# A hybrid trunk in fp32 on one core: five instead of four groups of a feed-forward by seven products, and loads, norms and low parts placed anew

## The chip, the core and the metric

One core of a Trainium2 chip. The time is the device time of one execution in microseconds (us), the median of several. TensorE (PE) multiplies, VectorE (DVE) adds and subtracts, ScalarE (ACT) copies and applies functions, GpSimd (POOL) does powers and some subtractions and issues DMAs, SyncE (SP) issues the loads.

## The reference

Sequence 512, width 1024, two layers. Layer 0 mixes with an mLSTM, layer 1 with a gMLP. Each layer is feed-forward, mixer, feed-forward, embedding; every step is a residual with a layer norm.

```python
D_MODEL = 1024; SEQ = 512; DEPTH = 2; FFN_HIDDEN = 2816; DN_ALPHA = (2.0 * DEPTH) ** 0.25
def swiglu_ffn(x, w_gu, w_d):
    g, u = jnp.split(x @ w_gu, 2, axis=-1)
    return (jax.nn.silu(g) * u) @ w_d
def gmlp_mixer(x, w_in, b_in, vn_g, vn_b, ws, bs, w_out):
    u, v = jnp.split(jax.nn.gelu(x @ w_in + b_in, approximate=False), 2, axis=-1)
    v = layer_norm(v, vn_g, vn_b).reshape(B, NB, GM_BLOCK, GM_GROUPS, GM_GDIM)
    ...
    s = jnp.einsum('gts,bnsgc->bntgc', ws_m, v) + bs.T[:, :, None]
    return (u * s.reshape(B, S, GM_WIDTH)) @ w_out
...
    for i in range(DEPTH):
        x = layer_norm(DN_ALPHA * x + 0.5 * swiglu_ffn(x, ffn1_wgu[i], ffn1_wd[i]), ln_g[i, 0], ln_b[i, 0])
        j = i // N_MIXERS
        if i % N_MIXERS == 0:
            mix = mlstm_mixer(x, ml_w_in[j], ml_b_in[j], ml_conv[j], ml_norm_g[j], ml_w_out[j])
        else:
            mix = gmlp_mixer(x, gm_w_in[j], gm_b_in[j], gm_vn_g[j], gm_vn_b[j], gm_ws[j], gm_bs[j], gm_w_out[j])
        x = layer_norm(DN_ALPHA * x + mix, ln_g[i, 1], ln_b[i, 1])
        x = layer_norm(DN_ALPHA * x + 0.5 * swiglu_ffn(x, ffn2_wgu[i], ffn2_wd[i]), ln_g[i, 2], ln_b[i, 2])
        ple = jax.nn.sigmoid(x @ ple_wg[i] + ple_bg[i]) * (p[i] @ ple_wp[i])
        x = layer_norm(DN_ALPHA * x + ple, ln_g[i, 3], ln_b[i, 3])
```

## The kernel before, in words

The activation x stays on the chip as `xt` (four token blocks of 128 tokens, t = 0 to 3, by 1024). For a matrix product over its columns a block is turned on PE (`turn_x`, four 128x128 transposes for each half into `xps`) and split into a high and a low part, `xh` and `xl`, in the type fp32r. Every product in fp32 is three products of such parts (`mm3`, lines 258 to 260): high by high, high by low, low by high. The norm behind the first feed-forward of a layer and behind a mixer is "deferred": only mean and scale are applied to `xt` (L535), gain and bias when a block is turned (`xf` on ACT). The others multiply with `g_bc` and add `b_bc` in two operations for each half (L538, L539).

The program is scheduled by hand: each engine runs its instructions in the order in which the code issues them.

`Weights` (`W`) holds one list of all weight tiles in the order of their use. `fill` takes them strictly in that order: it splits a loaded tile (`wraw`, or `wquarter` for the quarters of a group) into `whi` on ACT (L183) and `wlo` on DVE (L189), and stops at the first tile whose kind has no free buffer. The kinds are "main" (4 buffers), "extra" (2) and, in a feed-forward, "rows" (3). With `low="dma"` the low part is made by an ACT copy and an accumulating DMA of POOL (L186, L187), with `low=pool` by a subtraction on POOL. `release` frees a buffer and fills again; `release(later=True)` keeps it for a `refill`.

A feed-forward has 22 hidden blocks of 128 columns. Each takes two projections (`fps`, 24 matmuls of 512 columns), then silu, the product `hf` and its split. They go down to `xt` in chunks of 2, 4, 4, 4, 4, 4 blocks. The first 2 and the last 4 go plainly (`down`: for each token block two banks `dps`, 24 matmuls for each hidden block). Each chunk of four in the middle is a `Group`: its 2 by 2 product is made by seven products of quarters instead of eight (`product(r)`, 12 matmuls into two banks `gps`; even r uses one pair of banks, odd r the other), with `form()` making the sums of h on DVE and their split (`fhi`, `flo`), and `add()` adding a product's two banks to `xt`. The products of a group stand between the projections of the next chunk: each follows one projection. The weights of the products come as "rows" tiles, one behind each of the next chunk's projection tiles in `W`'s list.

Behind the last chunk `down` runs token block by token block: `residual` and `norm.stats` for both halves, then `norm.prepare` (aggregate, `rs`, a power on POOL) and `norm.scale`, and the turns of the block two places before. Turns of the last blocks are `hooks` that the next stage runs inside its first projections (`up_staged`).

At the start x's blocks and the first weights are loaded in turn. In the gMLP the v half is projected first (`gvps`, `up_tokens`), normed and split (`gvh`, `gvl`), then u (`gups`) and the mixing over tokens (`sps`). In the embedding a block is worked in `(t, e)` steps: `rest()` of one step runs behind the sigmoid of the next.

Of the kernel before, what the change touches and what calls it, by code (L numbers as in the profile page):

```python
# [16 lines left out]
P = 128  # L17
D = 1024
# [28 lines left out]
class Weights:  # L47
# [68 lines left out]
    def reserve(self, kind, n):  # L116

        js = [self.add_load(None, 1, kind) for _ in range(n)]
        self.held_raws[kind].extend(js)
        return js, [self.spare(kind) for _ in js]  # L120

    def spare(self, kind):
        return self.raw_pools[kind].tile([P, 1024], F32R, name="wquarter", tag="wquarter")

    def drop(self, js):
        for j in js:
            self.left[j] = 0
# [9 lines left out]
    def load(self, only=None):  # L137

        for kind, queue in self.queues.items():
# [3 lines left out]
            if queue and len(held) < self.raw_bufs.get(kind, 0) and only in (None, kind):  # L143
# [9 lines left out]
                for i in range(parts):  # L153
                    s = slice(i * a // parts, (i + 1) * a // parts)
                    self.nc.sync.dma_start(raw[:, s], ap[:, s])
# [72 lines left out]
def hybrid_trunk(ctx: ExitStack, tc, x, p, ln_g, ln_b, ffn1_wgu, ffn1_wd, ffn2_wgu, ffn2_wd,  # L228
# [80 lines left out]
    FFN_CHUNKS = [2, 4, 4, 4, 4, 4]  # L309
    LAST = len(FFN_CHUNKS) - 1  # L310
    turn_p = []

    def ffn_weights(wgu, wd, name, ple=False):
# [16 lines left out]
        for c, n in enumerate(FFN_CHUNKS):  # L330
            down_w = deque(forms(starts[c - 1]) if c > 1 else ())
            for i in range(2 * n):
                W.order.append(tiles[2 * starts[c] + i])
                if down_w:
                    W.order.append(down_w.popleft())
                if c == 1 and i == 1:
                    add_rows(wd, 0, n // 2, "rows")
# [166 lines left out]
    class Norm:  # L504
# [12 lines left out]
        def stats(self, t, i, n):  # L517

            if i == 0:
# [11 lines left out]
        def scale(self, t):  # L531
# [5 lines left out]
            for c in (slice(0, 512), slice(512, D)):  # L537
                vec.scalar_tensor_tensor(y[:, c], y[:, c], mean, self.g_bc[:, c], op0=OP.subtract, op1=OP.mult)  # L538
                vec.scalar_tensor_tensor(y[:, c], y[:, c], rstd, self.b_bc[:, c], op0=OP.mult, op1=OP.add)  # L539
# [42 lines left out]
    def down(hs, first, norm=None, low=(None,) * 4, between=None, lazy=False, defer=False):  # L582


        n = len(hs)
        ws, kinds = [], []

        def release(k):
            kind = "rows" if kinds[k] == "rows" else None
            if norm is None:  # L590
                W.release(kind=kind, low=low[k])
            elif kind == "rows":
                W.free[kind] += 1
            elif defer:
                W.release()
            else:
                W.release(later=lazy or bool(W.held))
# [3 lines left out]
        for t in range(TB):  # L601
            banks = [dn_bank("dps"), dn_bank("dps")]
            for k in range(n):
                if k == len(ws):
                    ws.append(W.take())
                    kinds.append(W.kind)
                if norm is not None and k == 1 and t:
                    norm.prepare(t - 1)
                    if t >= 2:
                        turn_x(t - 2, up_bank, (0,), norm)  # L610
                        if not norm.deferred:
                            turn_x(t - 2, up_bank, (1,), norm)
                    norm.scale(t - 1)
                if norm is not None and k == 2 and t >= 2 and norm.deferred:
# [12 lines left out]

            def finish(t=t, banks=banks):
                for half, ps in enumerate(banks):
                    residual(t, half, ps, first)  # L630
                    if norm is not None:
                        norm.stats(t, half, 2)
                if between is not None:
                    between(t)
                if norm is not None and t == TB - 1:
                    norm.apply(t)
                    set_hooks(norm)

            if defer and t == TB - 1:
                return finish  # L640
            finish()
            if first:
                run_affine()
# [8 lines left out]
    def up_staged(first=False):  # L652
# [37 lines left out]
    class Group:  # L690
# [5 lines left out]
        def __init__(self, h, pool):  # L696
            self.h, self.pool = h, pool
# [3 lines left out]
        def form(self):  # L701
# [4 lines left out]
            r = self.next_form  # L706
            if r == 7:
                return
            self.next_form += 1
# [22 lines left out]
        def add(self):  # L732
# [3 lines left out]
            for e, ps in enumerate(self.banks[r % 2]):  # L736
                residual(2 * i + e, j, ps, False)


    def ffn(layer, k, rows, prepare=None):  # L740
        with stage_pool("forms", 2) as fpool, stage_pool("quarters", Q_BUFS) as qpool, stage_pool("hpool", 2) as hpool:
            name = (layer, k)
            W.open_raw(name, qpool, Q_BUFS)
            reserved, hs = W.reserve(name, FFN_CHUNKS[0])
# [12 lines left out]
            pending = group = None  # L757
            for c, n in enumerate(FFN_CHUNKS):
                plain = c in (0, LAST)
                if c == 0:  # L760
                    hs = [halves(a) for a in hs]
                elif c == LAST:
                    assert not W.queues[name]
                    hs = []
                    if prepare is not None:
                        prepare()
                else:
                    h = hpool.tile([P, 4, SEQ], F32, name="h", tag="h")
                for i in range(2 * n):
# [8 lines left out]
                    else:  # L778
                        hf = tmp_tile("hf") if plain else h[:, b]
                        if c == LAST:  # L780
                            hs.append(halves(W.spare(name)))
                        vec.scalar_tensor_tensor(hf, sg, 0.5, ps, op0=OP.mult, op1=OP.mult)
                        if plain:
# [6 lines left out]
                    if (c, i) in ((0, 3), (1, 0)):  # L790
                        run_affine()
                    if i == 1 and pending is not None:
# [563 lines left out]
```

## Time and profile before

| | |
|---|---|
| median of 3 runs | 2259.32 us (2258.81 to 2259.34) |
| profiled execution | 2260.95 us, span 2259.1 us, mean granted clock 0.998 |
| PE busy | 2233.4 us, 99% of the span |
| DVE, ACT, POOL busy | 1448.7, 872.3, 121.2 us |
| DMA | 246.19 MB, mean 109 GB/s |

Rows of the time line read: start in us, duration, engine and line, operation, out<-in, sizes, how many like it in a row, and in brackets the idle time ahead with what ended it. Rows of waits read: who waits for what, then us in total, times, the longest. A row of windows has the stretch, its length, and the busy time and number of instructions of PE, PEld (weight loads), DVE, ACT and POOL, then the granted clock of PE, the DMA share and GB/s.

### The profile page before, as it was taken

The numbers are of one execution on the slowest core, as the hardware profiler recorded it, in microseconds if no ns is written. First come the engines' busy times: TensorE is split into PE (matmuls) and PEld (weight loads), VectorE is DVE, ScalarE is ACT, GpSimd is POOL, SyncE is SP. The second block draws the span as 40 slices with busy tenths as digits, with TensorE's granted clock in tenths as the row PEclk, the third lists the DMA queues.
The fourth block names the chain that finished last, engine by engine and source line by source line (L and its number), as shares of the span: only waits on it lengthen the run. The fifth ranks groups of instructions, "written<-read, shape, count | busy, mean of one in ns | idle before, by whom it ended". The sixth has DMA issues, their size and how long they took to land.

```text
span 2259.1 us, 26267 instructions
## 1 busy us (share of the span) xinstructions
PE 2233.4 (99%) x10623; PEld 1873.0 (83%) x10623; DVE 1448.7 (64%) x2083; ACT 872.3 (39%) x1226; POOL 121.2 (5%) x136
## 2 busy tenths in 40 slices
PE   8999999999999999999999999999999999999997
PEld 7888888888888888888888888888888888888886
DVE  4566667755555666666677566666666566666677
ACT  3333336454545433333254333335233352333332
POOL 1000000111111000000000000000021200000000
PEclk9999999999999999999999999999999999999999
DMA  7333223376684434331233322223223243332221
GB/s 236 104 96 100 94 84 103 78 175 126 145 163 102 147 112 142 101 103 66 94 122 125 121 91 87 91 94 117 89 94 103 75 137 98 129 112 85 84 84 56
DMA packets 192176, 246.19 MB, mean 109 GB/s; under 512 B 5380, under 2 KB 147844, under 8 KB 192056
## 3 DMA queue, kind: packets, MB, share of 16 engines
q1 hardware_dynamic: 165824, 211.83, 28.7%
q0 software_dynamic: 19616, 18.01, 5.6%
q10 hardware_dynamic: 6616, 14.69, 1.9%
q8 instruction: 83, 1.36, 0.2%
q14 instruction: 37, 0.30, 0.0%
HBM read 224.58 MB, written 2.11 MB: 100 GB/s over the span
## 4 chain that ended last, share of the span: by engine, by line
PE 89%; DVE 6%; ACT 2%; DMA 1%; issue 1%; POOL 0%; SPq 0%; POOLq 0%; ACTq 0%; DVEq 0%
PE fps L258 13%; PE fps L260 13%; PE fps L259 13%; PE gps L260 5%; PE gps L259 5%; PE gps L258 5%; PE dps L258 4%; PE dps L260 4%; PE dps L259 4%; DVE wlo L189 2%; PE vps L258 1%; PE zps L258 1%; PE zps L260 1%; PE vps L259 1%; PE vps L260 1%; PE zps L259 1%
## 5 line engine op out<-in xcount | busy, mean ns | idle before, releaser
L258 PE MATMUL fps<-xh,whi 128*128 128x512 f32 x1312 | 510.6, 389 | 0.0
L259 PE MATMUL fps<-xl,whi 128*128 128x512 f32 x1312 | 510.5, 389 | 0.0
L260 PE MATMUL fps<-xh,wlo 128*128 128x512 f32 x1312 | 510.4, 389 | 0.0
L189 DVE TENSOR_TENSOR wlo<-wraw,whi 128x1024 fp32r<-128x1024 f32 (+1 forms) x284 | 341.2, 1218 | 185.0 <-ACT whi L183 184.1
L183 ACT ACTIVATE whi<-wraw 128x1024 fp32r<-128x1024 f32 (+1 forms) x333 | 343.5, 1048 | 217.5 <-PE fps L259 103.1
L260 PEld LDWEIGHTS fps<-xh,wlo 128*128 128x128 f32 x1312 | 246.3, 188 | 51.1
L259 PEld LDWEIGHTS fps<-xl,whi 128*128 128x128 f32 x1312 | 246.3, 188 | 51.0
L258 PEld LDWEIGHTS fps<-xh,whi 128*128 128x128 f32 x1312 | 246.3, 188 | 50.9
L189 DVE TENSOR_TENSOR wlo<-wquarter,whi 128x1024 fp32r<-128x1024 f32 x112 | 137.3, 1226 | 201.8 <-ACT whi L183 201.8
L183 ACT ACTIVATE whi<-wquarter 128x1024 fp32r<-128x1024 f32 x112 | 118.6, 1059 | 237.7 <-PE gps L260 177.7
L260 PE MATMUL gps<-whi,flo 128*128 128x512 f32 x448 | 174.3, 389 | 0.0
L258 PE MATMUL gps<-whi,fhi 128*128 128x512 f32 x448 | 174.3, 389 | 0.0
L259 PE MATMUL gps<-wlo,fhi 128*128 128x512 f32 x448 | 174.3, 389 | 0.0
L776 ACT ACTIVATE sg<-fps 128x512 f32<-128x512 f32 x80 | 48.0, 600 | 282.4 <-PE fps L260 282.4
L556 DVE TENSOR_TENSOR xt<-xt,gps 128x512 f32<-128x512 f32 x224 | 143.2, 681 | 0.0
L263 ACT ACTIVATE fhi<-h 128x512 fp32r<-128x512 f32 x112 | 69.5, 625 | 115.9 <-DVE h L712 45.8
L528 POOL TENSOR_TENSOR rs<-rs,eps_pow 128x1 f32<-128x1 f32 x32 | 20.3, 636 | 1575.5 <-DVE rs L527 1575.5
L258 PE MATMUL dps<-whi,hh 128*128 128x512 f32 x256 | 101.6, 397 | 0.7 <-ACT hh L263 0.7
L259 PE MATMUL dps<-wlo,hh 128*128 128x512 f32 x256 | 100.5, 393 | 0.0
L260 PE MATMUL dps<-whi,hl 128*128 128x512 f32 x256 | 100.5, 392 | 0.0
L264 DVE TENSOR_TENSOR flo<-h,fhi 128x512 fp32r<-128x512 f32 x112 | 75.7, 688 | 36.4 <-ACT fhi L263 36.4
L259 PEld LDWEIGHTS gps<-wlo,fhi 128*128 128x128 f32 x448 | 84.1, 188 | 17.5
(276 smaller groups left out, 3942.5 us busy)
## 6 DMA issues: line engine op xcount, KB each, us to landing
wraw<-in_ffn_wgu_dram SPq DMA_DIRECT2D x80, 1024.0 KB, 5.3
wquarter<-in_ffn_wd_dram SPq DMA_DIRECT2D x64, 512.0 KB, 3.8
wraw<-in_ml_w_in_dram SPq DMA_DIRECT2D x24, 1024.0 KB, 5.7
wlo<-wraw POOLq DMA_DIRECT2D x34, 512.0 KB, 7.8
wraw<-in_gm_w_in_dram SPq DMA_DIRECT2D x15, 1024.0 KB, 5.6
wraw<-in_ffn_wd_dram SPq DMA_DIRECT2D x12, 1024.0 KB, 5.0
wraw<-in_ml_w_out_dram SPq DMA_DIRECT2D x8, 1024.0 KB, 5.3
wraw<-in_ple_wg_dram SPq DMA_DIRECT2D x8, 1024.0 KB, 5.2
```

Source lines behind the costliest of these rows:

```text
L183: self.nc.scalar.activation(hi[:, s], src[:, s], AF.Copy)
L189: (low or self.nc.vector).tensor_sub(lo[:, s], src[:, s], hi[:, s].bitcast(F32))
L258: mm(ps, st[0], mv[0], start=start, stop=False, skip_group_check=more)
L259: mm(ps, st[0], mv[1], start=False, stop=False, skip_group_check=more)
L260: mm(ps, st[1], mv[0], start=False, stop=stop, skip_group_check=more)
L263: sca.activation(hi, src, AF.Copy)
L264: vec.tensor_sub(lo, src, hi.bitcast(F32))
L528: pool.tensor_tensor(rs[:, 1:2], rs[:, 0:1], eps_pow, op=OP.pow)
L556: vec.tensor_add(dst, dst, ps)
L776: sca.activation(sg, ps, AF.Silu)
```

## The change

The chunks of a feed-forward become 4, 4, 4, 4, 4, 2: five groups go by seven products and the last two blocks plainly. Products 0 to 3 of the last group stand beside the last four projections; 5, 4 and 6 (in that order) come behind them in a new function `last_down`, among the plain parts of the last two blocks, some of which add into a product's banks. The norms and turns of this stretch are written into it. The chunk of two at the beginning with its reserved buffers is gone. Of the rest: the first two blocks of x are loaded ahead of all weights and the first weight tiles in halves; 26 transposes of `ident` into an unused bank stand among the first turns (`warm`); the hooks of `up_staged` stand at other places; a full norm does both products with the gain before the two with the bias; the embedding runs `rest()` at once for t < 3 and `norm.apply(t - 1)` behind the first sum of block t; in the gMLP low parts that POOL subtracted come by ACT and a POOL DMA, and the last two buffers of each v quarter are given back later.

```diff
-    FFN_CHUNKS = [2, 4, 4, 4, 4, 4]
+    FFN_CHUNKS = [4, 4, 4, 4, 4, 2]
+    LAST_ORDER = (0, 1, 2, 3, 5, 4, 6)
...
-        add_rows(wd, starts[LAST], 4, ["rows", "rows", "main", "main"] if ple else ["main", "rows", "rows", "rows"])
+        add_rows(wd, starts[LAST], 2, ["main", "main"] if ple else ["main", "rows"])
+        W.order.extend(down_w[r - 4] for r in LAST_ORDER[4:])
...
-    nc.sync.dma_start(xt[:, 0], x[0, 0:P, :])
+    load_x(0, 2)
     W.load()
-    nc.sync.dma_start(xt[:, 1], x[0, P:2 * P, :])
     W.load()
-    for t in (2, 3):
-        nc.sync.dma_start(xt[:, t], x[0, t * P:(t + 1) * P, :])
-    W.load()
+    W.load(between=lambda: load_x(2, TB))
...
-            for c in (slice(0, 512), slice(512, D)):
+            parts = slice(0, 512), slice(512, D)
+            for c in parts:
                 vec.scalar_tensor_tensor(y[:, c], y[:, c], mean, self.g_bc[:, c], op0=OP.subtract, op1=OP.mult)
+            for c in parts:
                 vec.scalar_tensor_tensor(y[:, c], y[:, c], rstd, self.b_bc[:, c], op0=OP.mult, op1=OP.add)
...
-                up(ps, w, 0, 256, (((0, 4), (2, 6)) if first else ((6,), (2,)))[i - 1])
+                up(ps, w, 0, 256, (((0,), (2, 7)) if first else ((), (0, 3)))[i - 1])
...
+    def last_down(hs, group, norm, lazy, defer):
+        ws, kinds = [], []
+        def part(t, half, ps, more):
+            for k in range(2):
+                mm3(ps, [a[:, t * P:(t + 1) * P] for a in hs[k]],
+                    [a[:, 0, half * 512:(half + 1) * 512] for a in ws[k]], k == 0 and not more, k == 1, more)
+        def take(t, half, ps):
+            residual(t, half, ps, False)
+            norm.stats(t, half, 2)
+        def own(t, half):
+            ps = up_bank("dps")
+            part(t, half, ps, False)
+            return ps
+        def turn(t, half):
+            turn_x(t, up_bank, (half,), norm)
+        x, y = group.banks
+        group.add()
+        for _ in range(2):
+            ws.append(W.take())
+            kinds.append(W.kind)
+        for t in range(2):
+            take(t, 0, own(t, 0))
+        group.product(5)
+        group.form()
+        part(0, 1, y[0], True)
+        take(0, 1, y[0])
+        group.product(4)
+        norm.prepare(0)
+        group.add()
+        norm.scale(0)
+        part(1, 1, y[1], True)
+        take(1, 1, y[1])
+        group.product(6)
+        turn(0, 0)
+        norm.prepare(1)
+        ps = own(2, 1)
+        turn(0, 1)
+        norm.scale(1)
+        part(2, 0, x[0], True)
+        take(2, 1, ps)
+        take(2, 0, x[0])
+        turn(1, 0)
+        norm.prepare(2)
+        ps = own(3, 1)
+        turn(1, 1)
+        norm.scale(2)
+        part(3, 0, x[1], True)
...
-                    up_tokens(t, ws, ps, hook=run_hook if t else None)
+                    up_tokens(t, ws, ps, hook=run_hook if t else None, release=give_back)
...
+                    if c and t < 2:
+                        W.refill()
...
-                W.release(low=pool)
+                W.release(low="dma")
+            W.refill(2)
...
-                    W.release(low=pool if b < 14 else None)
+                    W.release(low="dma" if b < 14 else None)
...
+                        if t and e == 0:
+                            norm.apply(t - 1)
                         rest()
...
                             norm.stats(t, e, n)
-                            if e == n - 1:
-                                norm.apply(t)
+                        if t < TB - 1:
+                            rest()
+                            rest = lambda: None
...
+    warm(16)
     turn_x(0)
     W.fill(1)
     turn_x(1)
+    warm(10)
     W.fill(1)
```

`give_back` in the gMLP releases a quarter's first two buffers at once and its last two with `later=True`. Lines 258 to 260, 183, 189, 535, 538, 539 and 556 of before are 255 to 257, 180, 186, 535, 539, 541 and 558 after the change.

The end of the first feed-forward on DVE, before: the last projection's product `hf_2497` and its split, the low part of the last tile, and then the down pass, whose `dps` blocks are taken (residual, BN_STATS) and scaled one by one (xt_86 is x, h_1651 the h of a group).

```order
L556 TENSOR_TENSOR xt_86<-xt_86,gps_2103 128x512
L556 TENSOR_TENSOR xt_86<-xt_86,gps_2104 128x512
L782 SCALAR_TENSOR_TENSOR hf_2497<-sg_2440,fps_2470 128x512
L264 TENSOR_TENSOR wquarter_2498<-hf_2497,wquarter_2498 128x512
L189 TENSOR_TENSOR wlo_2503<-wraw_2359,whi_2502 128x1024
L556 TENSOR_TENSOR xt_86<-xt_86,dps_2506 128x512
L521 BN_STATS st_2533<-xt_86 128x6
L556 TENSOR_TENSOR xt_86<-xt_86,dps_2507 128x512
L521 BN_STATS st_2533<-xt_86 128x6
L525 BN_AGGR mv_2545<-st_2533 128x2
L527 TENSOR_SCALAR rs_2547<-mv_2545 128x1
L535 TENSOR_SCALAR xt_86<-xt_86,mv_2545,rs_2547 128x1024
```

Here every group product has been added before the down pass begins.

The same place on DVE after the change, from the last split of `hf`: `wlo_2536` is the low part of product 4's weights, gps_2417 and gps_2418 are the banks of product 3 and then of product 5, and the two `dps` banks are the first plain parts.

```order
L838 SCALAR_TENSOR_TENSOR hf_2518<-sg_2468,fps_2491 128x512
L261 TENSOR_TENSOR wquarter_2520<-hf_2518,wquarter_2520 128x512
L186 TENSOR_TENSOR wlo_2536<-wquarter_1947,whi_2535 128x1024
L700 TENSOR_TENSOR h_1899<-h_1899 128x2x256
L261 TENSOR_TENSOR flo_2541<-h_1899,fhi_2540 128x512
L558 TENSOR_TENSOR xt_86<-xt_86,gps_2417 128x512
L558 TENSOR_TENSOR xt_86<-xt_86,gps_2418 128x512
L558 TENSOR_TENSOR xt_86<-xt_86,dps_2546 128x512
L521 BN_STATS st_2554<-xt_86 128x6
```

Two adds of a product now stand behind the low part of a product's weights and the forming of a sum, and ahead of the plain parts.

Further on in the same queue, after the change: `wlo_2579` is the low part of product 6's weights, the three `wlo` of `wraw` are the mixer's first main tiles, gps_2355 and gps_2356 are the banks of product 4 and then of product 6.

```order
L186 TENSOR_TENSOR wlo_2579<-wquarter_2064,whi_2578 128x1024
L186 TENSOR_TENSOR wlo_2583<-wraw_2266,whi_2582 128x1024
L186 TENSOR_TENSOR wlo_2587<-wraw_2266,whi_2586 128x1024
L186 TENSOR_TENSOR wlo_2593<-wraw_2318,whi_2592 128x1024
L261 TENSOR_TENSOR flo_2597<-h_1899,fhi_2596 128x512
L558 TENSOR_TENSOR xt_86<-xt_86,gps_2417 128x512
L521 BN_STATS st_2554<-xt_86 128x6
L525 BN_AGGR mv_2620<-st_2554 128x2
L527 TENSOR_SCALAR rs_2622<-mv_2620 128x1
L558 TENSOR_TENSOR xt_86<-xt_86,gps_2355 128x512
L558 TENSOR_TENSOR xt_86<-xt_86,gps_2356 128x512
L535 TENSOR_SCALAR xt_86<-xt_86,mv_2620,rs_2622 128x1024
```

The mixer's tiles stand ahead of the adds of product 4 and the first scale.

More of the change, by code (lines that the diff above doesn't have):

```diff
@@ L580, in set_hooks, with down @@
             affine.extend([lambda t=t: norm.finish(t) for t in range(TB)])
-    def down(hs, first, norm=None, low=(None,) * 4, between=None, lazy=False, defer=False):
+    def down(hs, first, norm=None, low=(None,) * 4, between=None):
         n = len(hs)
-        ws, kinds = [], []
+        ws = []
         def release(k):
-            kind = "rows" if kinds[k] == "rows" else None
             if norm is None:
[L591 to L595, printed above, removed]
+                W.release(low=low[k])
             else:
-                W.release(later=lazy or bool(W.held))
+                W.release(later=bool(W.held))
                 if not W.held:
@@ L626, in down @@
                             release(j)
[L628 to L635, printed above, removed]
-                    norm.apply(t)
[L637 to L643, printed above, removed]
+            for half, ps in enumerate(banks):
+                residual(t, half, ps, first)
+                if norm is not None:
+                    norm.stats(t, half, 2)
+            if between is not None:
+                between(t)
+        if norm is not None:
+            norm.apply(TB - 1)
+            set_hooks(norm)
     def up(ps, w, t0=0, t1=SEQ, hooked=()):
@@ L736, in add, with finish, give_back @@
             for e, ps in enumerate(self.banks[r % 2]):
-                residual(2 * i + e, j, ps, False)
+                residual(2 * i + e, j, ps, r in self.first)
+    def last_down(hs, group, norm, lazy, defer):
[6 more added lines that the diff above has]
+            residual(t, half, ps, False)
+            norm.stats(t, half, 2)
+        def own(t, half):
[36 more added lines that the diff above has]
+        part(3, 0, x[1], True)
+        def finish():
+            take(3, 1, ps)
+            take(3, 0, x[1])
+            norm.prepare(3)
+            if not defer:
+                give_back()
+            norm.scale(3)
+            set_hooks(norm)
+        def give_back():
+            for kind in kinds:
+                if kind == "rows":
+                    W.free[kind] += 1
+                elif defer:
+                    W.release()
+                else:
+                    W.release(later=lazy)
+        if defer:
+            give_back()
+            return finish
+        finish()
     def ffn(layer, k, rows, prepare=None):
@@ L803, in ffn @@
                     norm = Norm(layer, k)
-            return down(pending, False, norm, lazy=layer == 0, defer=prepare is not None)
+            return last_down(hs, group, norm, lazy=layer == 0, defer=prepare is not None)
     def ffn_stage(layer, k):
@@ L1316, in ffn_ple, with warm @@
                     set_hooks(norm)
+    def warm(n):
+        ps = up_bank("warm")
+        for _ in range(n):
+            nc.tensor.transpose(ps[:, :P], ident, ident)
+    warm(16)
     turn_x(0)
```

83 lines of the change are left out of this document (36 added, 47 removed).

## The prediction

> **What bounds the kernel now.** I read the page's first lines, then PE's waits, a window in the steady part, and the time lines around one seven-product group and the end of one feed-forward (FFN).
>
> ```profile
> span 2259.1 us, 26267 instructions
> PE 2233.4 (99%) x10623; PEld 1873.0 (83%) x10623; DVE 1448.7 (64%) x2083; ACT 872.3 (39%) x1226; POOL 121.2 (5%) x136
> ...
> PE xps L426 <- DMA xt<-in_x_dram: 6.9, 2, 4.7
> PE xps L426 <- DVE xt L535: 3.2, 4, 1.4
> PE sps L1189 <- ACT gvh L263: 1.6, 1, 1.6
> PE sup L260 <- DVE wlo L189: 0.8, 1, 0.8
> PE dps L258 <- ACT hh L263: 0.7, 1, 0.7
> PE gvps L259 <- DVE wlo L189: 0.5, 1, 0.5
> PE sps L1190 <- DVE gvl L264: 0.3, 1, 0.3
> PE sup L258 <- ACT whi L183: 0.3, 1, 0.3
> ...
> 200.00:300.00 100.00, 100.00 (x443) 82.84 (x442) 64.91 (x77) 34.88 (x42) 0.00 (x0) 1.00 0.22 71
> ```
>
> PE works for 99% of the span; its waits (us in total, times, longest) sum to 14.3 us, and the largest is the first load of x. So time goes only with PE work or these waits, and it comes with every new wait of PE. Window 200:300 holds 443 matmuls of 512 columns in 100 us: 0.2257 us each.
>
> **The saved matmuls.** Each FFN computes 96 + 5x84 = 516 down matmuls of 512 columns instead of 6x24 + 4x96x7/8 = 528: 12 fewer, 48 in all, 48 x 0.2257 = 10.8 us, all on PE's path: 2.7 per FFN.
>
> **What it pays: the end of each FFN.** How long a seven-product group takes to turn over its banks shows in the middle of before's first FFN:
>
> ```profile
> 304.68 0.39 PE L258 MATMUL fps<-xh,whi 128*128 128x512 f32 x1
> 310.12 0.39 PE L258 MATMUL gps<-whi,fhi 128*128 128x512 f32 x1
> ...
> 304.88 1.06 ACT L183 ACTIVATE whi<-wquarter 128x1024 fp32r<-128x1024 f32 x1 [2.12 <-PE gps L260]
> 309.03 0.63 ACT L263 ACTIVATE fhi<-h 128x512 fp32r<-128x512 f32 x1 [2.14 <-DVE h L714]
> ...
> 305.97 1.23 DVE L189 TENSOR_TENSOR wlo<-wquarter,whi 128x1024 fp32r<-128x1024 f32 x1 [3.58 <-ACT whi L183]
> 307.12 1.22 DVE L189 TENSOR_TENSOR wlo<-wraw,whi 128x1024 fp32r<-128x1024 f32 x1
> 308.25 0.68 DVE L714 TENSOR_TENSOR h<-h 128x512 f32<-128x512 f32 x1
> 309.69 0.69 DVE L264 TENSOR_TENSOR flo<-h,fhi 128x512 fp32r<-128x512 f32 x1 [0.76 <-ACT fhi L263]
> 310.30 1.28 DVE L556 TENSOR_TENSOR xt<-xt,gps 128x512 f32<-128x512 f32 x2
> ```
>
> A product ends at 304.68 and frees a "rows" buffer. Then, one behind the other: whi on ACT, two wlo, h, fhi on ACT, flo, and the adds that empty the product's two banks; the first add ends at about 310.30 + 0.65 = 310.95, 6.3 us after the product. Today that costs nothing, because a projection of 24 matmuls (304.68 to 310.12) and a product on the other banks lie between.
>
> In the new `last_down` no projection is left. With T = 0 at the end of product 3 (the same PE work is done as at the first dps of before, 342.76), PE has two dps groups, 12 matmuls, 2.7 us, and then product 5 on product 3's banks. DVE has the chain above with one wlo fewer (6.3 - 1.15 = 5.1). Stall one: 2.4 us. The other durations are in before's down pass and, the last two rows, in its last norm:
>
> ```profile
> 342.76 0.39 PE L258 MATMUL dps<-whi,wquarter 128*128 128x512 f32 x1
> ...
> 347.72 0.69 DVE L556 TENSOR_TENSOR xt<-xt,dps 128x512 f32<-128x512 f32 x1 [0.89 <-PE dps L260]
> 348.44 0.69 DVE L521 BATCH_NORM_STATS2 st<-xt 128x6 f32<-128x512 f32 x1
> ...
> 350.49 0.21 DVE L525 BATCH_NORM_AGGREGATE mv<-st 128x2 f32<-128x12 f32 x1
> 350.73 0.15 DVE L527 TENSOR_SCALAR rs<-mv 128x1 f32<-128x1 f32 x1
> 351.58 0.81 DVE L535 TENSOR_SCALAR xt<-xt,mv,rs 128x1024 f32<-128x1024 f32 x1 [0.70 <-POOL rs L528]
> ...
> 357.91 0.69 DVE L435 TENSOR_TENSOR xl<-xf,xh 128x512 fp32r<-128x512 f32 x1 [1.59 <-ACT xh L434]
> 358.52 0.81 DVE L535 TENSOR_SCALAR xt<-xt,mv,rs 128x1024 f32<-128x1024 f32 x1
> ...
> 355.00 0.60 PE L426 MATMUL xps<-ident,xt 128*128 128x128 f32 x4
> 366.42 0.60 PE L426 MATMUL xps<-ident,xt 128*128 128x128 f32 x4
> ...
> 355.70 1.51 ACT L431 ACTIVATE xf<-xps,cols 128x128 f32<-128x128 f32 x4 [10.13 <-PE xps L426]
> 357.25 0.64 ACT L434 ACTIVATE xh<-xf 128x512 fp32r<-128x512 f32 x1
> ...
> 2253.60 0.75 DVE L539 SCALAR_TENSOR_TENSOR xt<-xt,rs,b_bc 128x512 f32<-128x512 f32 x1 [0.44 <-POOL rs L528]
> 2255.05 0.75 DVE L539 SCALAR_TENSOR_TENSOR xt<-xt,rs,b_bc 128x512 f32<-128x512 f32 x1
> ```
>
> A take (residual and statistics) is 1.33 us, aggregate with rs 0.4, a scale 0.8 after 0.7 on POOL, xf with xh 2.1, xl 0.65. Behind its adds DVE has two takes, to T = 8.4. Then stands the wlo of product 6's weights, whose whi waits for the end of product 5 (5.1 + 2.7 = 7.8), as only two rows buffers are left to the products; and behind it, in the same queue, three wlo of the next stage's main tiles, flo, a take, aggregate and rs, and only then the adds of product 4, for which product 6 waits. From 7.8: whi 1.1, four wlo 4.7, flo 0.7, take 1.3, rs 0.4, one add 0.65 = 8.8, T = 16.6. PE has 24 matmuls in that time (5.4, to 13.2). Stall two: 3.4 us.
>
> Product 6 ends at 19.4. Then turn(0,0), dps, turn(0,1), part, and turn(1,0), which waits for scale(1). PE needs 3.7 us for the work between (12 matmuls, 2.7, and two turns of about 0.48); DVE stands behind the first turn's xl (2.1 + 0.65), rs, the second turn's xf and xh (2.1 more on ACT) and its xl, then the scale: 6.5. Stall three: 2.8. The same pattern once more, takes and two xl before scale(2), gives stall four before turn(2,0): 2.7. Sum 11.3 in this FFN, and the same in layer 1's first (there the last is a main tile's wlo behind the takes). The two FFNs ahead of an embedding have two main tiles behind product 5 instead of three (stall two 2.3); their turns have no xf, but three operations of 0.75 of a scale come before a turn (stall three 2.1); and at the fourth place other PE work comes first. That is 6.8 each. Together 36.2 us, less the 10.8 saved: +25.4 us. Each stall is a sum of rows, good to about 0.5 us.
>
> **The clock.** What a stall leaves behind is seen once, after the waits of 1.6 and 0.3 us of sps:
>
> ```profile
> 1200.00:1204.00 4.00, 2.83 (x24) 2.83 (x25) 2.02 (x3) 3.22 (x9) 0.26 (x1) 1.00 0.00 0
> 1650.00:1654.00 4.00, 2.05 (x13) 1.39 (x12) 2.96 (x5) 2.39 (x4) 0.19 (x1) 1.00 0.26 87
> 1654.00:1658.00 4.00, 4.00 (x16) 3.47 (x16) 3.43 (x6) 2.84 (x5) 3.64 (x2) 0.57 0.04 9
> ...
> 1656.16 0.63 PE L260 MATMUL gups<-xh,wlo 128*128 128x512 f32 x1
> 1656.58 0.63 PE L258 MATMUL gups<-xh,whi 128*128 128x512 f32 x1
> ```
>
> Granted clock 0.57 in the next 4 us, matmuls every 0.42 us: 4 x 0.43 = 1.7 us lost. After 1.4 us (window 1200:1204) it stayed at 1.00. The 14 stalls above, 2.2 to 3.4 us each, are all longer than the two waits together that brought the drop. The bounds are 0 and 14 x 1.7 = 24 us; a slower PE also fills part of the next stall, which DVE's queue sets. I take half, 12 us, because the one drop seen came beside small matmuls of 256 columns, which these are not.
>
> The Trainium skill ("TensorE: Matmul & The Clock Gate", "HAM oscillation — how this bites in real kernels") asks for PE gaps over about 3.4 us before it speaks of a drop. By that rule hardly any of the 14 drops the clock, and the 12 us are left out; the trace's drop after 1.6 and 0.3 us speaks against the rule.
>
> **The rest of the change.** Start: x's first two tiles go ahead of all weights, with SP's queue issuing the weights later. The second wait for x (6.9 - 4.7 = 2.2) goes and the two sup waits (1.1) may; w1 and w2 are now late instead. The 26 dummy transposes lie in time in which PE waits for loads. Bounds: a loss of 1 and a gain of 3.3; I take -1.6. Mixer of layer 1: 13 low parts go from POOL's subtraction to ACT and a POOL DMA, two to DVE, and the held weights come back later, so that ACT and DVE are free for gvh and gvl: the waits of 1.6, 0.3 and 0.5 go (2.4), and with them the clock's 1.7; ACT has slack (39%). Bounds 0 and -4.1; I take -4.0. Transposes of the first projection: the waits of 3.2 on xt and 0.7 on hh are the ones that the new places of the hooks can change; I give back about 0.4 at four stages, for turn(3,1) now comes late in the third projection: -1.6, bounds +2 and -3.9. End: DVE's backlog behind PE sets it (its last operation begins at 2255.05). The rest of a block now runs before the next block's sigmoid (about 1.4 us less queued), and both products with g_bc lie in the 0.44 us wait for rs: -1.9, bounds 0 and -2.5. Sum -9.1. The additional DVE and ACT work of the fifth group lies beside PE's matmuls (DVE 64%, ACT 39%) and costs nothing before the tail. If that cover failed, it would show as waits of gps inside the groups.
>
> **Sum.** On the profiled execution's span: 2259.1 + 25.4 - 9.1 + 12 = 2287.4. That execution took 2260.95 us, 1.6 above the median of 2259.32; on the median 2259.32 + 28.3 = 2288.
>
> **Rivals.**
> (a) The stalls come and the clock stays: 2276. For it: one drop alone is seen, among small matmuls, and 1.4 us brought none. Against it: each stall is longer than what brought that one.
> (b) The tails are covered, and the kernel gets faster: the adds of products 3 and 4 and the scales end before PE comes to them. That is -10.8 - 9.1, 2240, or some 2250 with half of one stall per FFN. It decides below 10.8 + 9.1 = 20 us of stalls, 1.4 per place instead of 2.6. For it: before's down pass has DVE idle between its takes (0.89 us before 347.72), and a scale that a slot further on would be early enough. Against it: the chain of 6.3 us is measured, and the main tiles' wlo stand in front of the adds.
> (c) The stalls are half as long and the clock stays: about 2258, no change.
> (d) Every stall drops the clock at full price: 2300.
> (e) The new places of loads and hooks do nothing or harm, with the stalls as in the forecast: 2288 + 5 to 9 us, 2293 to 2297.
>
> **Chances.** Forecast 0.40, (a) 0.28, (b) 0.13, (c) 0.06, (d) 0.05, (e) 0.08. Below 0.2% (4.5 us) a measurement of this kernel can hardly tell a change from none. Faster 0.15, same 0.04, slower 0.81. The range 2263 to 2298 leaves out (b), most of (c) and (d). The likeliest case alone would be 2280 to 2296.
>
> **What would show it.** In the changed trace, PE's waits name gps<-xt adds and xps<-xt scales at the end of all four FFNs, 2 to 3.4 us each and 36 in all, with a granted clock under 0.8 behind many of them; no sps wait remains; the first sup begins 1 to 2 us earlier; the span between PE's last matmul and the end is 2 us shorter. If gps at product 5 doesn't wait, the chain was mis-read and (b) holds. If the stalls are there and the clock is 1.00 behind them, (a) holds.

## The result, and the profile after

| | median us | runs | ratio to before, 95% interval |
|---|---|---|---|
| before | 2259.07 | 2257.90 to 2259.34 (4) | |
| changed | 2300.44 | 2295.85 to 2302.88 (4) | 1.0179 [1.0167, 1.0192] |

The change makes the kernel 41.4 us slower. Its direction and its mechanism were forecast; the time lies 2.4 us above the range and 12 us above the number. The profiled execution is the fastest of the four (2295.85 us); the others were granted a mean clock of 0.989 to 0.991, it 0.993.

The first lines of the page of the changed kernel, and PE's waits (us in total, times, longest):

```profile
span 2294.1 us, 26402 instructions
PE 2240.9 (98%) x10601; PEld 1874.4 (82%) x10601; DVE 1494.1 (65%) x2149; ACT 905.9 (39%) x1263; POOL 101.4 (4%) x134
...
PE gps L255 <- DVE xt L558: 21.0, 8, 3.5
PE xps L426 <- DVE xt L535: 7.9, 4, 2.6
PE xps L426 <- DVE xt L541: 4.0, 2, 2.0
PE gps L257 <- DVE flo L261: 3.1, 3, 1.0
PE gvps L256 <- DVE wlo L186: 2.2, 1, 2.2
PE sps L1249 <- DVE gvl L261: 1.9, 1, 1.9
PE warm L1388 <- POOL ident masks.py:199: 1.4, 1, 1.4
PE sup L256 <- DVE xl L435: 1.1, 5, 0.3
PE dps L255 <- ACT hh L260: 0.7, 1, 0.7
PE sup L652 <- ACT xh L434: 0.5, 1, 0.5
```

Eight waits of gps on the adds (L558), four and two of a turn on a scale (L535, L541). Before, no gps waited at all. PE has 22 instructions fewer and yet 7.5 us more busy time: it ran part of the time at half speed. Windows of 4 us behind the first and second stall of the first feed-forward, and behind the same two of the second (span, busy times by engine, then PE's granted clock):

```profile
346.00:350.00 4.00, 4.00 (x13) 3.17 (x12) 2.49 (x4) 0.00 (x0) 0.00 (x0) 0.66 0.01 4
359.00:363.00 4.00, 4.00 (x11) 3.17 (x12) 2.32 (x4) 0.00 (x0) 0.00 (x0) 0.58 0.02 6
1129.00:1133.00 4.00, 4.00 (x20) 3.28 (x19) 2.91 (x5) 1.61 (x2) 0.00 (x0) 1.00 0.00 0
1141.00:1145.00 4.00, 4.00 (x23) 3.35 (x22) 3.33 (x7) 1.20 (x2) 0.46 (x1) 1.00 0.00 0
```

The first two stalls (2.33 and 3.46 us) dropped the clock, the last two (2.33 and 2.34 us) did not. Of the 14 stalls of this execution 8 did.

### The profile page after: what moved, and what is told of

The parts are those of the page before. It is cut to its first block, busy times and chain, and to the rows that moved or that the text cites. A ratio compares the mean times of both kernels' runs of the same rounds, so it can differ in the third digit from the quotient of the medians.

```text
span 2294.1 us, 26402 instructions
## 1 busy us (share of the span) xinstructions
PE 2240.9 (98%) x10601; PEld 1874.4 (82%) x10601; DVE 1494.1 (65%) x2149; ACT 905.9 (39%) x1263; POOL 101.4 (4%) x134
## 4 chain that ended last, share of the span: by engine, by line
PE 88%; DVE 5%; ACT 3%; issue 2%; DMA 1%; POOL 0%; SPq 0%; DVEq 0%; ACTq 0%; POOLq 0%
PE fps L255 13%; PE fps L256 13%; PE fps L257 12%; PE gps L255 6%; PE gps L257 6%; PE gps L256 6%; PE dps L255 3%; PE dps L257 3%; PE dps L256 3%; DVE wlo L186 1%; PE zps L255 1%; PE zps L257 1%; PE zps L256 1%; PE gvps L256 1%; PE gvps L257 1%
## 5 line engine op out<-in xcount | busy, mean ns | idle before, releaser
L186 DVE TENSOR_TENSOR wlo<-wquarter,whi 128x1024 fp32r<-128x1024 f32 x140 | 171.6, 1225 | 268.7 <-ACT whi L180 268.7
L180 ACT ACTIVATE whi<-wquarter 128x1024 fp32r<-128x1024 f32 x140 | 148.4, 1060 | 334.9 <-PE gps L257 248.8
L255 PE MATMUL gps<-whi,fhi 128*128 128x512 f32 x560 | 221.7, 396 | 21.0 <-DVE xt L558 21.0
L257 PE MATMUL gps<-whi,flo 128*128 128x512 f32 x560 | 220.3, 393 | 3.1 <-DVE flo L261 3.1
L256 PE MATMUL gps<-wlo,fhi 128*128 128x512 f32 x560 | 220.3, 393 | 0.0
L558 DVE TENSOR_TENSOR xt<-xt,gps 128x512 f32<-128x512 f32 x248 | 159.0, 680 | 0.0
L260 ACT ACTIVATE fhi<-h 128x512 fp32r<-128x512 f32 x140 | 86.8, 625 | 150.0 <-DVE h L698 57.2
L255 PEld LDWEIGHTS gps<-whi,fhi 128*128 128x128 f32 x560 | 106.6, 190 | 46.3 <-issue 13.2
L257 PEld LDWEIGHTS gps<-whi,flo 128*128 128x128 f32 x560 | 106.7, 190 | 26.9 <-DVE flo L261 4.4
L256 PEld LDWEIGHTS gps<-wlo,fhi 128*128 128x128 f32 x560 | 106.8, 191 | 21.9
L261 DVE TENSOR_TENSOR flo<-h,fhi 128x512 fp32r<-128x512 f32 x140 | 94.6, 688 | 45.8 <-ACT fhi L260 45.8
```

Of the source, the lines that this page charges most:

```text
L180: self.nc.scalar.activation(hi[:, s], src[:, s], AF.Copy)
L186: (low or self.nc.vector).tensor_sub(lo[:, s], src[:, s], hi[:, s].bitcast(F32))
L255: mm(ps, st[0], mv[0], start=start, stop=False, skip_group_check=more)
L256: mm(ps, st[0], mv[1], start=False, stop=False, skip_group_check=more)
L257: mm(ps, st[1], mv[0], start=False, stop=stop, skip_group_check=more)
L260: sca.activation(hi, src, AF.Copy)
```

## The experiments

Each ran five rounds beside the kernel before. Diffs are against the kernel that the text names.

**The parts apart.** The first leaves the groups as they were and takes the rest of the change; the second takes the groups alone.

```diff
 e1_others: all hunks of the change except FFN_CHUNKS, ffn_weights, down, Group, last_down, ffn
 e2_groups: these hunks alone, with the helpers of Weights and Norm.stats that they need
```

> The kernel before with everything of the change except the feed-forward's groups: loads, dummy transposes, hook places, norm order, embedding order, gMLP low parts and releases. Theory (these parts gain, the groups' tail loses): start -2.7, hooks -1.6, end -2.1, gMLP between 0 and -4, so 2249 to 2253 us, and no wait of PE over 1 us outside the start and the gMLP. Rival (part of the loss comes from these parts, by the low parts that went from POOL to ACT and DMA): 2262 us or more, with new waits in the gMLP.

> The kernel before with the feed-forward's part alone (five groups by seven products, last_down), everything else as before. Theory: 14 stalls of 2 to 3.5 us in the four ends (34.6 us), three waits of 1.04 us on flo, about 0.2 us more at each for refilling PE, 10.8 us of matmuls saved, some 11 clock drops of 1.65 us: 2304 to 2312 us. Rival (the other parts add to the loss): 2290 us or less.

Measured: 2252.51 us, 0.9971 [0.9961, 0.9982], and 2303.75 us, 1.0200 [1.0186, 1.0214], the second 0.25 us below what was expected. Against before's 2258.88 us in the same rounds the first is 6.4 us faster and the second 44.9 us slower, so the loss is all in the groups' part. PE's waits of the first:

```profile
PE sps L1207 <- DVE gvl L269: 1.9, 1, 1.9
PE warm L1346 <- POOL ident masks.py:199: 1.4, 1, 1.4
PE sup L676 <- ACT xh L441: 1.4, 1, 1.4
PE sup L264 <- DVE xl L442: 1.0, 5, 0.3
PE dps L263 <- ACT hh L268: 0.7, 1, 0.7
```

No wait of a turn on a scale is left (3.2 us before). The 1.9 us in the gMLP has taken the place of three waits of 2.4 us.

**The clock.** Only dummies of PE are added, in the stalls:

```diff
 e3_busy, against the changed kernel
+        busy(22)          # transposes of ident into a free bank
         group.product(5)
...
+        busy(24)
         group.product(6)
...
+        busy(18)
         turn(1, 0)
```

> The changed kernel with dummy transposes of ident into a free bank ahead of product 5 (22), of product 6 (24) and of the turn of block 1 (18) in each feed-forward, while PE waits there; what PE waits for is left as it is. Theory (a stall of over 2 us drops the granted clock by half for about 3.4 us): the named stalls become short and the clock stays at 1.00 behind 12 of the 14, about 9 drops of 1.65 us less in the median: 2283 to 2289 us, and the runs lie within 3 us instead of 7. Rival (the clock costs nothing that the stalls don't hide): 2299 us or more.

Measured: 2286.55 us (2285.74 to 2288.37). Behind the first two stalls of the first feed-forward:

```profile
346.00:350.00 4.00, 4.00 (x19) 3.32 (x18) 2.91 (x5) 1.70 (x2) 0.00 (x0) 1.00 0.00 0
357.00:361.00 4.00, 3.87 (x19) 3.28 (x20) 2.59 (x4) 0.41 (x2) 0.05 (x1) 1.00 0.08 31
```

The clock is 1.00, the kernel 13.9 us faster though PE does more work and waits for the same things, and the spread fell from 7 to 2.6 us. So the drops, with what refilling PE costs, take 14 us of the median at these three places of each feed-forward alone.

**DVE's order, step by step.** Each of these builds on the one before it.

```diff
 e4_addfirst, against the changed kernel (last chunk, i == 3)
-                        group.product(i)
+                        group.product(i, hold=last)   # hold: no W.release
+                        if last:
+                            group.add()
+                            W.release(kind="rows")
                         group.form()
...  in last_down
-        group.add()
 e5_dmamains
-        group.product(5)
+        group.product(5, hold=True)
+        W.free["rows"] += 1
+        W.fill(1)
...
-        group.product(4)
+        group.product(4, hold=True)
+        W.free["rows"] += 1
+        W.fill(low="dma")
...
 e6_scalefirst
+        norm.prepare(1)
+        norm.scale(1)
         turn(0, 0)
-        norm.prepare(1)
         ps = own(2, 1)
+        take(2, 1, ps)
         turn(0, 1)
-        norm.scale(1)
...
+        norm.prepare(2)
+        norm.scale(2)
         turn(1, 0)
...
 e7_best
-                    if c == 0 and i > 2:
+                    if c == 0 and i > 1:
                         run_affine()
```

> The changed kernel with the adds of the last group's product 3 ahead of the split of product 4's weights on DVE; nothing else moved. Theory (DVE's order makes product 5 wait): the first stall of 2.33 us is gone in all four feed-forwards, and the second grows by about 0.7 us, as product 5 starts earlier and DVE's queue does not: -9.4 + 2.8, and some three drops of 1.65 fewer: 2287 to 2291 us. Rival (product 5 waits for its weights or for ACT, not for the adds): 2299 to 2301 us with the first stall unchanged.

> The kernel of the run before (adds of product 3 ahead), and now the next stage's first tiles, which stood on DVE behind product 5, get their low parts from ACT and a POOL DMA behind product 4; rows buffers are given back without a fill there. Theory (three, or two, subtractions of 1.17 us ahead of product 4's adds make the second stall): the second stall goes from 3.8 and 2.67 us to about 0.6 in all four feed-forwards, -10.6 us, some three clock drops fewer (-5), and gvps no longer waits for a low part (-2): 2269 to 2275 us. Rival (the low parts come late by DMA and the next stage waits for them, or product 6 waits for its own weights): 2281 us or more, with new waits on wlo.

Measured: 2288.09 and 2272.93 us, both as the theory has it. Waits of gps on the adds in the first, then in the second:

```profile
PE gps L255 <- DVE xt L558: 12.9, 4, 3.8
...
PE gps L255 <- DVE xt L558: 1.6, 4, 0.4
```

From 21.0 us in eight waits to 12.9 in four (the second stall grew to 3.8, as a fixed queue must make it) and to 1.6. So the stalls are DVE's queue: the low parts of weights ahead of the adds.

> As the run before, and in last_down the aggregate and scale of a block stand ahead of the low parts of the turned block before it, and the takes of blocks 2 and 3 as early as their banks allow; PE's order is unchanged. Theory (the scale waits behind two xl): the third stall (2.5 and 2.0 us) goes to under 0.5 in all four, the fourth (2.3 in the first feed-forward) shrinks by about 1, some four clock drops fewer: 2253 to 2259 us. Rival (the turn waits for the aggregate, so for its own block's last product, wherever the scale stands): 2268 us or more.

> As the run before, and gain and bias of the deferred norm are applied one projection earlier in a feed-forward's first chunk, so that none stands ahead of the fourth block's product h. Theory (the wait of 1.04 us on flo at the first product of three feed-forwards comes from there): these three waits go, -3.5 us: 2247 to 2255 us, faster than before. Rival (flo waits for the split of the weights): the three waits stay, no change against the run before.

Measured: 2266.75 and 2264.49 us: 6 us instead of some 16, then 2.3. The three waits on flo are gone in the second. The first missed by what the moved scales hold up: the third stalls went and the fourth shrank as expected, but new waits of 5.3 us came, of pwp, the embedding's first product (4.1 us), and of dps (1.2 us) on xl, because ahead of an embedding a scale is four operations, and the turned block's xl now stood behind them; gvps waited 0.5 us longer. Two waits at the first turn (1.9 and 1.2 us), which I had not foreseen either, came with the run before it: the block's power stands on POOL behind the tiles' DMAs, and DVE's scale behind the power (POOL's and DVE's time line of e5_dmamains):

```profile
349.77 1.62 POOL L184 DMA_DIRECT2D wlo<-wraw  x1 [335.19 <-ACT wlo L183]
351.66 1.54 POOL L184 DMA_DIRECT2D wlo<-wraw  x1 [0.26 <-DVE xt L558]
353.55 1.52 POOL L184 DMA_DIRECT2D wlo<-wraw  x1 [0.35 <-ACT wlo L183]
354.45 1.23 POOL L528 TENSOR_TENSOR rs<-rs,eps_pow 128x1 f32<-128x1 f32 x1
...
355.72 0.81 DVE L535 TENSOR_SCALAR xt<-xt,mv,rs 128x1024 f32<-128x1024 f32 x1 [3.54 <-POOL rs L528]
```

**The gMLP's low parts.**

```diff
 e8_nogmlp: e1_others without the three gMLP hunks
 e10_othersbusy, against e1_others
                     mm(ps, vh[:, t], wsp[:, g], start=True, stop=False)
+                    if (b, t) == (0, 0):  # 18 transposes of ident
```

> Loads, dummy transposes, hook places, norm order and embedding order of the change, without its groups and without its gMLP part (low parts on POOL as before). Theory (the gMLP part only trades waits: 2.4 us and a clock drop of 1.6 against one wait of 1.9): 2254 to 2256 us against 2252.5 with it. Rival (it gains the 4 us that I had forecast): 2256.5 us or more; rival (it gains nothing): 2252.5 us.

> The kernel without the groups' part (2252.5 us), with 18 dummy transposes behind the gMLP's first matmul of the token mixing, in the 1.87 us in which PE waits for gvl. Theory (that wait drops the clock in about half of the runs): 1 to 1.7 us less, 2250.8 to 2251.5 us, with no granted clock under 0.95 in the stretch behind. Rival (no drop there, or it is hidden): 2252.5 us or more.

Measured: 2253.41 us (2251.88 to 2254.01) and 2251.90 us (2251.51 to 2254.26), against 2252.51 (2251.52 to 2253.37). Both differences are 0.9 us or less and lie within the spreads. The gMLP part gains at most about 1 us. The dummies ran ahead of the wait on gvl and took up its time, without a gain that can be told from none: inconclusive.

**How far the end can be mended.**

```diff
 e9_poollow, against e7_best
-                            W.release(kind="rows")
+                            W.release(kind="rows", low=pool)
-        W.fill(1)
+        W.fill(1, low=pool)
-        W.fill(low="dma")
+        W.fill(1, low="dma")
...
         norm.scale(1)
+        W.fill(low="dma")
...  and scale(2) behind turn(1, 1) where the norm isn't deferred
 e11_r6pool:   product 4's low part on DVE again
 e12_earlyback: give_back() right behind part(3, 0), not in finish()
 e13_nopool:   product 6's low part on DVE again
```

> As the best of the runs before (2264.5 us), and in the end of each feed-forward the low parts of products 4 and 6 are subtracted on POOL instead of DVE, only one of the next stage's tiles is sent to POOL's DMA ahead of the first block's power, the others behind the second scale, and ahead of an embedding the third scale stands behind the turned block's low parts. Theory (DVE's and POOL's queues hold more work there than PE has to cover it): the waits of 0.4 at product 6, of 1.2 and 1.9 at the first turn and of 2.05 at pwp go, the 1.45 before the turn of block 2 goes to under 0.5: about 9 us and one or two clock drops, 2252 to 2256 us. Rival (POOL's subtraction of 2.6 us is too slow and makes new waits at products 4 and 6): 2263 us or more.

> As the run with low parts on POOL (2257.8 us), but only product 6's are made there; product 4's are subtracted on DVE again. Theory (POOL's 2.6 us for product 4's low part made product 4 late and so the adds before product 6: the 1.25 us waits): these four waits fall under 0.4, 4 x (0.9 + 0.25 for refilling PE) = 4.6 us less: 2252 to 2254.5 us. Rival (they come from product 6's own low part on POOL): the 1.25 us waits stay, 2257 us or more.

> As the run beside it, and the buffers of the last two blocks' weights are given back right behind their last matmul and not behind the takes of block 3. Theory (the fourth tile of the v projection is split too late, PE waits 2.6 us for it and the clock drops behind it in most runs): that wait goes, 2.6 + 0.25 + some 1.2 of the clock: 2248.5 to 2250.5 us, faster than the kernel without the groups' part (2252.5). Rival (the split stands ahead of block 3's scale, and the turn of block 3 waits instead): 2251 us or more with a new wait of 1 us or more on xt.

> As the run before (2255.5 us), with product 6's low part subtracted on DVE again, so that POOL does no subtraction in a feed-forward's end. Theory (the subtraction on POOL keeps a DVE operation of two SBUF inputs waiting: flo took 2.50 us beside it and 0.69 without): the 1.25 us wait ahead of product 6 falls to about 0.4 in all four, 3.4 us less: 2251 to 2253 us. Rival (the wait comes from ACT or from the weights): 2254.5 us or more, the 1.25 us wait unchanged.

Measured: 2257.78, 2257.85, 2255.45 and 2251.58 us. In e9 the waits at the first turn and at pwp went, but the 1.4 us before the turn of block 2 stayed, and product 6 waited 1.25 us in all four ends; in e11 it still did, so the rival held. In e12 the 2.6 us wait of gvps went, another of 0.6 us came later in the v projection, and 2.4 us of the 4 that I had named were gained. e13 brought product 6's wait back to 0.4 us and 3.9 us with it.

## Why the prediction was right or wrong, point by point

By stages, the profiled execution's difference against before, from the starts of the same PE work in both traces (the forecast's clock term has a row of its own, the measured one lies within the stages):

| stage | forecast us | measured us |
|---|---|---|
| start | -1.6 | -2.7 |
| first feed-forward, layer 0 | +8.6 | +13.6 |
| second, layer 0 | +4.1 | +6.2 |
| first, layer 1, with the v projection | +8.6 | +15.5 |
| second, layer 1 | +4.1 | +7.7 |
| token mixing of the gMLP | -4.0 | -2.0 |
| hooks, first projections, embedding | -1.6 | -1.1 |
| end, behind PE | -1.9 | -2.1 |
| clock | +12 | |
| sum | +28.3 | +35.0 |

**The matmuls saved, the stalls.** Right. (The totals of down matmuls in the forecast, 516 and 528, are added up wrongly: it is 48 + 5x84 = 468 instead of 6x24 + 4x84 = 480. Both traces show this for the second feed-forward, and the difference of 12 holds.) The stalls came at the named places with 2.33, 3.46, 2.55, 2.30 / 2.33, 2.34, 2.00 / 2.33, 3.48, 2.54, 2.20 / 2.34, 2.34, 2.01 us, 34.6 in all against 36.2. Reading the chain of one group in before's trace and walking it along the new queue gave each within 0.5 us.

**The clock: mis-sized.** I took half of 14 drops, 12 us. The profiled execution had 8 (8 x 1.7 = 13.6 us). The median run was granted 0.991 instead of 0.993, which over 2299 us is 4.6 us, or about three more drops, 11 in all; no trace of such a run shows where. That makes 18.7 us, 6.7 more than I took. My reason for half, the small matmuls beside the one drop of before, was wrong: the windows above show drops among matmuls of 512 columns. That half came near the 8 was luck; what decides is where a stall falls in time, as the last section works out. Rival (a), stalls without drops, is refuted by these windows and by e3. Rival (d), every drop at full price, named 2300 us and met the median by luck: not all 14 dropped, and it too lacked the costs that follow. Rival (e) is refuted by e1, (b) and (c) by the stalls themselves.

**Two costs that were missing, some 8 us and the larger part of the miss.** First, the cover of the fifth group. The forecast puts its additional work at nothing because DVE is busy for 64% of the time; it named the cover's failure and gave it no price. Three waits of 1.04 us on flo came, 3.1 us. DVE in the first chunk of the second feed-forward:

```profile
840.10 1.22 DVE L550 TENSOR_TENSOR xt<-xt,g_bc 128x1024 f32<-128x1024 f32 x1
841.35 1.23 DVE L551 TENSOR_TENSOR xt<-xt,b_bc 128x1024 f32<-128x1024 f32 x1
842.50 0.68 DVE L838 SCALAR_TENSOR_TENSOR h<-sg,fps 128x512 f32<-128x512 f32 x1
843.09 1.22 DVE L186 TENSOR_TENSOR wlo<-wraw,whi 128x1024 fp32r<-128x1024 f32 x1
844.23 1.29 DVE L261 TENSOR_TENSOR flo<-h,fhi 128x512 fp32r<-128x512 f32 x2
```

The last of the four deferred gains and biases stands ahead of the product h, from which the first sums are split; without it there the waits are gone (e7). Second, a stall costs more than its gap, by which alone the forecast prices it. The second feed-forward of layer 0 shows it without a drop (its first matmul and the first behind its end, before and after):

```profile
799.34 0.40 PE L258 MATMUL fps<-xh,whi 128*128 128x512 f32 x1
1133.98 0.39 PE L258 MATMUL pwp<-whi 128*128 128x512 f32 x1
...
810.65 0.40 PE L255 MATMUL fps<-xh,whi 128*128 128x512 f32 x1
1151.45 0.40 PE L255 MATMUL pwp<-whi 128*128 128x512 f32 x1
```

334.6 us became 340.8, 6.2 more. Its gaps (2.33, 2.34, 2.00, 1.04) less the 2.7 us of matmuls are 5.0; the other 1.2 us are about 0.3 for each of the four gaps. A matmul lasts 0.39 us and the next follows after 0.226, so 0.16 us of overlap is lost at each gap, and the second matmul behind a gap starts some 0.1 us late as well (0.34 us behind the first at 1128.27); why it does stays open. Over the 14 stalls and three waits on flo that is some 5 us, an estimate. With the 6.7 us of the clock the two costs come to about 2 us more than the 12 that the forecast was off, which the smaller differences of the table don't resolve.

**The rest.** The start gained more than I took (-2.7), within its bounds. The gMLP gained less, 2.0 us instead of 4.0: the waits on gvh went, and a wait of 1.9 us on gvl took their place. The hooks gained 0.5 us less than I took, and the end came as worked out: PE's last matmul and the last operation of DVE, before the change and after (before's last DVE row stands in the prediction):

```profile
2247.41 0.28 PE L260 MATMUL gps<-whi,xl 128*128 128x256 f32 x1
...
2284.50 0.28 PE L257 MATMUL gps<-whi,xl 128*128 128x256 f32 x1
...
2289.46 1.40 DVE L541 SCALAR_TENSOR_TENSOR xt<-xt,rs,b_bc 128x512 f32<-128x512 f32 x2
```

From PE's last start to the end of the span 11.7 us before, 9.6 after.

**The range.** Its upper end stood at 2298 because I gave every drop at full price 1 in 20. With the refill and the flo waits in the sum, the forecast would have been 2296 us with half of the drops and 2303 us with 11.

**What the groups are worth.** With the end mended (e13, 2251.58 us, 0.9963 [0.9950, 0.9977]) five groups cost the same as four with the rest of the change (e1, 2252.51 us). In the profiled executions of the two, the four feed-forwards (with the v projection) are together 2.6 us shorter in e13 instead of 10.8. Ten waits that e13 has there and e1 has not make up 5.4 us of the missing 8.2; the other 2.8 us are some 0.3 us of refilling for each, an estimate. Most of these waits are in three rows (one wait of 0.6 us in the first row lies outside the feed-forwards):

```profile
PE xps L426 <- DVE xt L535: 2.0, 2, 1.4
PE gps L255 <- DVE xt L558: 1.6, 4, 0.4
PE dps L255 <- DVE xl L435: 1.2, 2, 0.6
```

Both are faster than the kernel before and the changed one. Whether another order would free the rest of the 10.8 us stays open.

## What to carry to other kernels

Work that is taken off PE at a stage's end also takes away the cover of the queues behind it: count what each in-order engine has to do between the last covered point and PE's next need, in its own order, before counting matmuls saved. Put what PE waits for (adds that free a bank, scales) ahead of what only prepares the next stage. Here a PE gap of over 2 us cost its length, some 0.3 us of refilling, and, where most of it fell into one 3.4 us piece of the grid, 1.7 us of clock; if such a gap can't be removed, dummy work on PE in it pays (13.9 us here). A mean busy share of 64% does not say that an engine is ahead at the place where PE needs it.

## What the runs showed of the hardware

**When the clock drops.** Over the 15 traces of this case, gaps of PE counted behind 30 us, a drop being a granted clock under 0.95 from 1 us ahead of the gap's end to 5 us behind it (two places with two gaps close together left out, each of which dropped it: 1.61 + 0.34 and 1.39 + 0.34):

| gap us | gaps | with a drop |
|---|---|---|
| 0.25 to 1.6 | 115 | 0 |
| 1.6 to 1.95 | 14 | 9 |
| 1.95 to 2.4 | 31 | 10 |
| 2.4 to 2.8 | 16 | 12 |
| over 2.8 | 6 | 6 |

Eleven of the 14 gaps in the second row are at one place, the gMLP's sps among small matmuls. Nearly every drop shows the same 0.72 over these 6 us, 6 x 0.28 = 1.7 us lost, as 3.4 us at half speed would give. The table reads like a chance, and the traces show what lies behind it. The half-speed stretches of one trace begin on a fixed grid: in the changed kernel at 345.30, 358.96 and 369.20 us, four and three times 3.413 us apart, and so in every trace that has several. If a trace is cut along its grid, PE was idle for over half of the piece ahead of each of the 39 drops. No piece idle for less than 0.50 of its length was followed by a drop; of those from 0.50 to 0.57 12 of 21 were, and all 27 above. The same stall of 2.33 us shows both cases (windows of one piece each, in the changed kernel):

```profile
341.89:345.30 3.41, 1.15 (x6) 0.61 (x4) 2.65 (x5) 0.63 (x1) 0.00 (x0) 1.00 0.00 0
345.30:348.71 3.41, 3.34 (x8) 2.66 (x9) 3.19 (x6) 0.00 (x0) 0.00 (x0) 0.50 0.02 5
1123.55:1126.96 3.41, 2.38 (x11) 1.65 (x9) 1.86 (x3) 1.39 (x2) 0.00 (x0) 1.00 0.00 0
1126.96:1130.37 3.41, 2.10 (x9) 1.76 (x10) 3.38 (x6) 0.00 (x0) 0.00 (x0) 1.00 0.00 0
```

The first stall lies in one piece, in which PE worked for 1.15 of 3.41 us, and the clock is 0.50 in the next. The second is split over two pieces (2.38 and 2.10 us of work), and no drop follows.

The Trainium skill ("TensorE: Matmul & The Clock Gate", "What's actually happening") speaks of a free-running window of about 3.4 us, which agrees with the grid and with the length. Its rule that only gaps over about 3.4 us matter ("HAM oscillation — how this bites in real kernels") does not agree: 1.87 us was enough in 8 of 11 cases.

**POOL's subtraction holds up DVE.** DVE's and POOL's time line of e11, then the same DVE operation in e13 without POOL's subtraction:

```profile
347.66 2.50 DVE L261 TENSOR_TENSOR flo<-h,fhi 128x512 fp32r<-128x512 f32 x1
...
347.20 2.41 POOL L186 TENSOR_TENSOR wlo<-wquarter,whi 128x1024 fp32r<-128x1024 f32 x1 [332.71 <-ACT whi L180]
...
348.58 0.68 DVE L261 TENSOR_TENSOR flo<-h,fhi 128x512 fp32r<-128x512 f32 x1
```

2.50 us instead of 0.68, and it ends 0.55 us behind POOL's operation; so it does beside all twelve such subtractions of e9 and e11. Work moved from DVE to an idle POOL so freed nothing here. The Trainium skill ("SBUF — State Buffer", "SBUF: two separate sides") says that a DVE operation with two SBUF inputs and a GpSimd operation that reads SBUF exclude each other; the trace agrees.
